# A two-layer encoder trunk: three of the second layer's four seven-product units get weight sums made on VectorE in the mLSTM layer and stored

## The chip, the core and the metric

One core of one Trainium2 chip runs the whole program. The time is device microseconds of an execution; "before" is the median of three runs.

## What is computed

Two layers over 256 positions of width 2048, all in float32. Layer 0 mixes by pooling and attention, layer 1 by a bidirectional mLSTM; each ends in a gated MLP with a width-3 convolution, which is where the change acts:

```python
def conv_ffn(x, w_up, conv_w, conv_b, w_down):
    u = x @ w_up
    up = jnp.pad(u, ((0, 0), (1, 1), (0, 0)))
    c = conv_w.astype(u.dtype)
    u = c[0] * up[:, :-2] + c[1] * up[:, 1:-1] + c[2] * up[:, 2:] + conv_b.astype(u.dtype)
    gate, val = jnp.split(u, 2, axis=-1)
    return (jax.nn.silu(gate) * val) @ w_down
...
for layer in range(DEPTH):
    h = rms_norm(x, norm_mix[layer])
    ...
    x = x + mixed
    x = x + conv_ffn(rms_norm(x, norm_ffn[layer]), w_up[layer], conv_w[layer], conv_b[layer], w_down[layer])
```

## The kernel before

All weights pass through one stream (`Stream`) of chunks, as a rule 128 partitions by 1024 floats (512 KB). SP loads a chunk into one of six raw buffers `w` (L93, L100; seven in the MLP). It is then split into a high part and a low part: ScalarE casts `w` to the high part (L164), VectorE subtracts that from `w` for the low part (L165); both stand in `hl`, of which there are four buffers (five in the MLP). TensorE takes three products for each weight block, high by high, high by low and low by high, all through the helper at L285. A chunk is 12 matmuls of 128x512 where the weights move, or 16 matmuls (eight of 512 columns and eight of 256) where they stand still. Loads are issued up to five chunks ahead (seven in the MLP) and splits two (three); the next load into a raw buffer waits until the last reader of that buffer is done, and SP works in order. The tile framework orders the instructions of VectorE, ScalarE, GpSimd and SP by a schedule of its own; TensorE's order is written out by hand.

The up-projection of the MLP has 44 tiles of gate and value columns, in six groups (`FCH`). Most tiles are plain (`up`). Four times in a layer, four tiles are done at once as a **unit** (`quads`): a product of 2 by 2 blocks with seven products for eight, which needs sums of activations and sums of weights. The activations' sums are made once a layer on VectorE and ScalarE (`sums`, L1003 to L1019). A unit has 28 chunks of six matmuls; they are woven into plain work, slot by slot (a slot is one plain chunk), by the table `UNITS`. An entry is (group, half, first slot, last slot, prepared or not). I call the four units of a layer first to fourth.

The weights' sums come in two ways. In a unit that is not prepared, VectorE adds inside the raw buffers before the split (`sums` of `Stream`, L144, L147, L149, L150), 32 adds of 128x512 a unit. In a prepared unit the sums lie in DRAM tiles `G`, eight pairs a unit, made ahead of time by DMAs alone: two copies DRAM to DRAM from SP (L118), two accumulating DMAs from GpSimd (L119) and two more within `G` (L123); `_make_steps` gives for each pair the load index at which its four steps go out. The chunks of a prepared unit are loaded from `G` and from the weights, as many bytes as otherwise.

In the mLSTM layer the stream feeds, for each of four head pairs, a value projection (tile `mv`), two query and two key projections (`mq`, `mk`) and an output-gate projection (`mo`), then the output projection (`op`, into which `mcat` goes). VectorE also does the gating: L904 and four reciprocals L906 for each head pair, then L910 and L920. The code holds, unused before, a third way to make sums: a pair of chunks marked "prep" in the stream (`_with_prep`, `is_prep`, `prepare`), which is loaded into two raw buffers, summed by four adds (L134) and stored to `G` by two DMAs from GpSimd (L135, L136).

Of the kernel before, what the change touches and what calls it, by code (L numbers as in the profile page):

```python
# [1241 lines left out]
def _down_chunks(w):  # L1242
# [6 lines left out]


UNITS = (
    ((2, 1, 18, 62, 0), (3, 1, 66, 94, 1), (4, 1, 98, 142, 0), (5, 1, 146, 174, 1)),
    ((2, 1, 18, 62, 0), (3, 1, 66, 94, 1), (4, 1, 98, 142, 0), (5, 1, 146, 174, 1)),
)


# [73 lines left out]
def _with_prep(seq, pairs, first, gap):  # L1330

    out = []
    for i, e in enumerate(seq):
        n, r = divmod(i - first, gap)
        if r == 0 and 0 <= n < len(pairs):
            key, q = pairs[n]
            out += [(("prep", 0, key), q[:, 0:1024]), (("prep", 1, key), q[:, 1024:2048])]
        out.append(e)
    return out


def _make_steps(pairs, places):

    make = {}
    for (key, q), (at, gap) in zip(pairs, places):
        for part in range(4):
            make.setdefault(at + part * gap, []).append((key, part, q))
    return make
# [105 lines left out]
```

## Time and profile before

| | |
|---|---|
| median of 3 runs | 2179.74 us (2179.56 to 2181.44) |
| profiled execution | 2179.59 us, of which 2177.8 us span of instructions |
| granted TensorE clock | 1.000 |
| TensorE, VectorE, ScalarE, GpSimd busy | 2164.5, 1711.6, 1277.6, 133.5 us |
| DMA | 533.18 MB, mean 245 GB/s |

The attention layer fills the span up to about 256 us, the first MLP up to 977, the mLSTM layer up to 1455, the second MLP the rest. In a line of groups stand source line, engine, operation, tiles written and read, count, busy time, mean of one in ns, then the engine's idle time before them and what ended it. In a list of waits stand the waiting engine, tile and line, then who ended the wait, with the total in us, the number of waits and the longest. A timeline row has start, length, engine, line, operation, tiles, count, and in brackets the idle time before it.

### The profile page before, as it was taken

To read this page: it belongs to the slowest core of one execution; us is meant where nothing else is said; L and a number is where in the kernel's file an instruction comes from. 1 tells how busy PE (TensorE), PEld (TensorE's weight loads), DVE (VectorE), ACT (ScalarE), POOL (GpSimd) and SP (SyncE) were. 2 spreads that over 40 slices of the span, in tenths; PEclk is the share of its full clock that TensorE was granted. 3 is DMA by queue.
4 is the path that set the end of the run, shared out by engine and by line. 5 is a ranking of instruction groups with operands and counts; after the bars stand their busy time and mean duration, and the time that the engine had idled before them with its cause. 6 is when DMAs were issued, how large, how long until landed. Compare 5 with 4: busy or idle time off the path is not lost.

```text
span 2177.8 us, 30504 instructions
## 1 busy us (share of the span) xinstructions
PE 2164.5 (99%) x11040; PEld 1838.1 (84%) x11040; DVE 1711.6 (79%) x2414; ACT 1277.6 (59%) x1808; POOL 133.5 (6%) x168
## 2 busy tenths in 40 slices
PE   9999999999999999999999999999999999999999
PEld 7888888888888888889888888888888888888887
DVE  7686699888798787866767676669888879979785
ACT  7665555666565575655555554556566656556663
POOL 0121101000000000001101010110000000000000
PEclk9999999999999999999999999999999999999999
DMA  8868879889978878769788777877876875767773
GB/s 324 245 217 249 236 234 295 276 264 293 301 235 287 272 232 250 262 202 253 219 248 226 238 229 219 265 223 222 269 244 223 258 247 202 258 232 233 251 232 126
DMA packets 157467, 533.18 MB, mean 245 GB/s; under 512 B 18715, under 2 KB 21059, under 8 KB 156291
## 3 DMA queue, kind: packets, MB, share of 16 engines
q1 hardware_dynamic: 139744, 493.66, 66.2%
q0 software_dynamic: 14496, 33.83, 10.5%
q10 hardware_dynamic: 3074, 3.75, 0.9%
q8 instruction: 86, 1.41, 0.3%
q14 instruction: 67, 0.54, 0.1%
HBM read 529.02 MB, written 69.25 MB: 275 GB/s over the span
## 4 chain that ended last, share of the span: by engine, by line
PE 92%; DVE 6%; issue 1%; ACT 1%; DMA 0%; ACTq 0%; SPq 0%; DVEq 0%
PE up L285 24%; PE dn L285 20%; PE p L285 13%; PE op L285 8%; PE mv L285 4%; PE mq L285 4%; PE mk L285 4%; PE mo L285 4%; PE qproj L285 3%; DVE hl L165 3%; PE pool L285 1%; PE vproj L285 1%; PE kproj L285 1%; ACT hl L164 1%; PE tr L1098 1%
## 5 line engine op out<-in xcount | busy, mean ns | idle before, releaser
L165 DVE TENSOR_TENSOR hl<-w,hl 128x1024 fp32r<-128x1024 f32 (+1 forms) x868 | 1045.0, 1216 | 334.9 <-ACT hl L164 328.1
L164 ACT CAST hl<-w 128x1024 fp32r<-128x1024 f32 (+1 forms) x867 | 897.7, 1048 | 643.7 <-PE up L285 115.8
L285 PE MATMUL up<-xx,hl 128*128 128x512 f32 (+1 forms) x3584 | 647.8, 337 | 0.0
L285 PEld LDWEIGHTS up<-xx,hl 128*128 128x128 f32 x3584 | 563.4, 188 | 87.7 <-DVE hl L165 0.4
L285 PE MATMUL dn<-hl,g 128*128 128x512 f32 x2064 | 492.7, 391 | 0.0
L285 PEld LDWEIGHTS dn<-hl,g 128*128 128x128 f32 x2064 | 385.2, 188 | 78.5
L285 PE MATMUL p<-hl,sx 128*128 128x512 f32 x768 | 206.7, 391 | 3.5 <-DVE hl L165 2.5
L285 PEld LDWEIGHTS p<-hl,sx 128*128 128x128 f32 x768 | 139.4, 188 | 30.6 <-DVE hl L165 3.8
L285 PE MATMUL p<-hl,xx 128*128 128x512 f32 x576 | 157.9, 391 | 4.6 <-DVE hl L165 4.6
L285 PEld LDWEIGHTS p<-hl,xx 128*128 128x128 f32 x576 | 104.5, 188 | 25.3 <-DVE hl L165 6.3
L119 POOL DMA_DIRECT2D G<-in_q x64 | 52.2, 816 | 984.7 <-DMA G<-in_q 972.8
L285 PE MATMUL mk<-xx,hl 128*128 128x512 f32 (+1 forms) x512 | 92.2, 338 | 0.0
L285 PE MATMUL mq<-xx,hl 128*128 128x512 f32 (+1 forms) x512 | 92.2, 338 | 0.0
L285 PE MATMUL mv<-hl,xx 128*128 128x512 f32 (+2 forms) x480 | 91.8, 351 | 0.0
L285 PE MATMUL op<-hl,cat 128*128 128x512 f32 x384 | 91.7, 394 | 0.0
L285 PE MATMUL mo<-hl,xx 128*128 128x512 f32 x384 | 90.6, 392 | 0.0
L285 PE MATMUL op<-hl,mcat 128*128 128x512 f32 x384 | 89.5, 392 | 0.0
L285 PEld LDWEIGHTS mq<-xx,hl 128*128 128x128 f32 x512 | 79.3, 188 | 11.5
L285 PEld LDWEIGHTS mk<-xx,hl 128*128 128x128 f32 x512 | 79.1, 188 | 11.3
L285 PEld LDWEIGHTS mv<-hl,xx 128*128 128x128 f32 x480 | 78.3, 189 | 11.2
L285 PEld LDWEIGHTS op<-hl,mcat 128*128 128x128 f32 x384 | 71.5, 188 | 14.6
L285 PEld LDWEIGHTS mo<-hl,xx 128*128 128x128 f32 x384 | 71.0, 188 | 14.2
(243 smaller groups left out, 1860.8 us busy)
## 6 DMA issues: line engine op xcount, KB each, us to landing
w<-in_up SPq DMA_DIRECT2D x224, 512.0 KB, 4.7
w<-in_dn SPq DMA_DIRECT2D x176, 512.0 KB, 4.6
w<-in_m_in SPq DMA_DIRECT2D x124, 512.0 KB, 5.2
w<-in_q SPq DMA_DIRECT2D x96, 512.0 KB, 4.8
G<-in_q SPq DMA_DIRECT2D x64, 512.0 KB, 5.7
w<-in_a_in SPq DMA_DIRECT2D x46, 512.0 KB, 6.1
G<-in_q POOLq DMA_DIRECT2D x64, 256.0 KB, 6.4
G<-G POOLq DMA_DIRECT2D x64, 256.0 KB, 7.2
```

What stands on the lines that cost most here:

```text
L119: pin(add.dma_start(G[r, 0:1024], src[r, 512:1536], accum_op=ALU.add))
L164: (self.nc.vector.tensor_copy if i + c == 0 else self.nc.scalar.copy)(hl[:, 0, c : c + n], w[:, c : c + n])
L165: self.nc.vector.tensor_sub(hl[:, 1, c : c + n], w[:, c : c + n], hl[:, 0, c : c + n].bitcast(F32))
L285: pe.matmul(out_, lhsT, rhs, start=start, stop=stop, skip_group_check=True)
L1098: pe.transpose(tr[:, j, t * P : t * P + P], src[:, c : c + P], ident)
```

## The change

Which units are prepared changes in both layers, and how they are prepared in layer 1. In layer 0 the second and fourth were prepared; now the first and third are, as before by DMAs alone, issued at other loads (in the attention layer and in the first third of the MLP). In layer 1 the second and fourth were prepared by DMAs; now the first, second and fourth are, by the "prep" chunks: 24 pairs, one pair ahead of every seventh chunk of the mLSTM layer's stream, from its first. The DMAs that made layer 1's sums between the end of the first MLP and the second are gone. The slots of the units move.

```diff
 UNITS = (
-    ((2, 1, 18, 62, 0), (3, 1, 66, 94, 1), (4, 1, 98, 142, 0), (5, 1, 146, 174, 1)),
-    ((2, 1, 18, 62, 0), (3, 1, 66, 94, 1), (4, 1, 98, 142, 0), (5, 1, 146, 174, 1)),
+    ((2, 1, 18, 57, 1), (3, 1, 61, 101, 0), (4, 1, 105, 131, 1), (5, 1, 135, 174, 0)),
+    ((2, 1, 18, 57, 1), (3, 1, 61, 90, 1), (4, 1, 94, 140, 0), (5, 1, 144, 174, 1)),
 )
...
     weights = att + ffn(0)
-    make = _make_steps(pairs[0], [(24 + 11 * k, 5) for k in range(8)] + [(len(att) + 30 + 24 * k, 12) for k in range(8)])
-    make.update(_make_steps(pairs[1], [(len(weights) - 20 + 14 * k, 7) for k in range(16)]))
-    weights = weights + ml + ffn(1)
+    make = _make_steps(pairs[0], [(24 + 10 * k, 5) for k in range(8)] + [(len(att) + 24 + 17 * k, 8) for k in range(8)])
+    weights = weights + _with_prep(ml, pairs[1], 0, 7) + ffn(1)
```

Three places in the order of instructions follow. First, VectorE at the start of the first unit of layer 1, before:

```order
L144 TENSOR_TENSOR w_13317<-w_13317 128x512
L1009 TENSOR_TENSOR v_13136<-v_13136 128x512
L1010 TENSOR_TENSOR v_13136<-v_13136 128x512
L982 TENSOR_TENSOR y_2_13305<-y_2_13305 128x256
L1012 SCALAR_TENSOR_TENSOR v_13136<-v_13136 128x512
L165 TENSOR_TENSOR hl_13429<-w_13317,hl_13429 128x1024
L1013 TENSOR_TENSOR v_13136<-v_13136 128x512
L450 TENSOR_TENSOR tb_up_3_13410<-up_3_13316,tb_up_3_13410 128x512
L165 TENSOR_TENSOR hl_13452<-w_13340,hl_13452 128x1024
L149 TENSOR_TENSOR w_13363<-w_13363,w_13317 128x512
```

The same engine and place now (`sx` and `v` are the activations' sums, `w` a raw chunk, `hl` its split):

```order
L1019 TENSOR_TENSOR sx_13116<-v_13304,sx_13116 128x4x128
L450 TENSOR_TENSOR tb_up_3_13571<-up_3_13480,tb_up_3_13571 128x512
L165 TENSOR_TENSOR hl_13614<-w_13505,hl_13614 128x1024
L1019 TENSOR_TENSOR sx_13116<-v_13304,sx_13116 128x4x128
L984 TENSOR_TENSOR g_0_13124<-y_2_13469,g_0_13124 128x256
L1014 TENSOR_TENSOR v_13304<-v_13304 128x512
L1019 TENSOR_TENSOR sx_13116<-v_13304,sx_13116 128x4x128
L165 TENSOR_TENSOR hl_13638<-w_13528,hl_13638 128x1024
L994 TENSOR_TENSOR tb_up_3_13571<-tb_up_3_13571,R_13239 128x512
L165 TENSOR_TENSOR hl_13659<-w_13550,hl_13659 128x1024
```

The adds into `w` (L144, L149) are gone from the place; the activations' sums stay.

Second, VectorE after the output-gate projection of the third head pair in the mLSTM layer, before:

```order
L165 TENSOR_TENSOR hl_11431<-w_11348,hl_11431 128x1024
L297 TENSOR_TENSOR re_h_11397<-re_h_11397,ry_h_11395 128x2
L904 TENSOR_SCALAR og_11440<-og_11440 128x2x256 x2
L906 RECIPROCAL og_11440<-og_11440 128x256 x2
L165 TENSOR_TENSOR hl_11453<-w_11365,hl_11453 128x1024
L906 RECIPROCAL og_11440<-og_11440 128x256
L165 TENSOR_TENSOR hl_11471<-w_11410,hl_11471 128x1024
L165 TENSOR_TENSOR hl_11493<-w_11429,hl_11493 128x1024
```

And now:

```order
L165 TENSOR_TENSOR hl_11535<-w_11500,hl_11535 128x1024
L297 TENSOR_TENSOR re_h_11487<-re_h_11487,ry_h_11485 128x2
L134 TENSOR_TENSOR w_11399<-w_11399 128x512
L134 TENSOR_TENSOR w_11399<-w_11399,w_11416 128x512
L134 TENSOR_TENSOR w_11416<-w_11416,w_11399 128x512
L904 TENSOR_SCALAR og_11544<-og_11544 128x2x256 x2
L134 TENSOR_TENSOR w_11416<-w_11416 128x512
L906 RECIPROCAL og_11544<-og_11544 128x256 x3
L165 TENSOR_TENSOR hl_11557<-w_11523,hl_11557 128x1024
L906 RECIPROCAL og_11544<-og_11544 128x256
L165 TENSOR_TENSOR hl_11575<-w_11528,hl_11575 128x1024
```

The four adds of a pair stand around L904, and three reciprocals, not two, come ahead of the next subtract.

Third, VectorE after the output-gate projection of the second head pair, now (the pair in `w_10638` and `w_10657`; `w_10830` is the chunk that is loaded into the buffer of `w_10638`):

```order
L910 TENSOR_TENSOR hn_10358<-hn_10358,og_10668 128x512
L134 TENSOR_TENSOR w_10638<-w_10638 128x512
L165 TENSOR_TENSOR hl_10745<-w_10712,hl_10745 128x1024
L165 TENSOR_TENSOR hl_10773<-w_10733,hl_10773 128x1024
L906 RECIPROCAL og_10668<-og_10668 128x256
L134 TENSOR_TENSOR w_10638<-w_10638,w_10657 128x512
L165 TENSOR_TENSOR hl_10791<-w_10738,hl_10791 128x1024
L920 SCALAR_TENSOR_TENSOR mcat_8748<-htr_10760,cst,mcat_8748 128x256
L910 TENSOR_TENSOR hn_10618<-hn_10618,og_10668 128x512
L134 TENSOR_TENSOR w_10657<-w_10657,w_10638 128x512
```

Nothing of these adds stood there before; `w_10638` is final after the second of them and can then be stored.

## The prediction

> **What bounds the kernel now.** I read the page's busy times and chain first, then who the weight loads of TensorE wait for, then the windows around those waits.
>
> ```profile
> PE 2164.5 (99%) x11040; PEld 1838.1 (84%) x11040; DVE 1711.6 (79%) x2414; ACT 1277.6 (59%) x1808; POOL 133.5 (6%) x168
> PE 92%; DVE 6%; issue 1%; ACT 1%; DMA 0%; ACTq 0%; SPq 0%; DVEq 0%
> ```
>
> TensorE carries 92% of the chain that ended last, and the change takes no matmul away: both versions have four units in each layer. So only TensorE's waits can be won. A matmul's modelled end hides a part of each wait; the weight load's row shows it better. Waits of the weight loads, in four windows in this order: 300 to 400 us (first unit of layer 0, three rows), 600 to 700 (its third unit), 1500 to 1600 (first unit of layer 1, two rows), 1800 to 1900 (its third unit).
>
> ```profile
> PEld p L285 <- DVE hl L165: 2.7, 4, 1.1
> PEld p L285 <- ACT hl L164: 0.5, 1, 0.5
> PEld up L285 <- DVE hl L165: 0.4, 1, 0.4
> ...
> PEld p L285 <- DVE hl L165: 1.7, 1, 1.7
> ...
> PEld p L285 <- DVE hl L165: 4.5, 4, 2.0
> PEld p L285 <- ACT hl L164: 0.9, 1, 0.9
> ...
> PEld p L285 <- DVE hl L165: 1.2, 1, 1.2
> ```
>
> That is 3.6, 1.7, 5.4 and 1.2 us, **11.9 us in all, the ceiling of any gain**. Every one stands in the first third of a unit whose sums are made on the spot; the two prepared units of each layer show none. Is that VectorE being full, or the sums themselves? Three windows of 24 us and the mLSTM layer (columns: length, then busy us of PE, PEld, DVE, ACT, POOL, clock, DMA share, GB/s):
>
> ```profile
> 472.00:496.00 24.00, 24.00 (x130) 20.42 (x129) 23.14 (x40) 18.73 (x32) 1.64 (x2) 1.00 0.91 270
> 352.00:376.00 24.00, 24.00 (x126) 20.48 (x126) 22.34 (x28) 14.68 (x19) 1.61 (x2) 1.00 0.96 312
> 1840.00:1864.00 24.00, 23.15 (x112) 19.28 (x111) 21.10 (x27) 13.70 (x17) 0.00 (x0) 1.00 0.67 227
> 976.00:1454.00 478.00, 478.00 (x2572) 412.49 (x2571) 330.67 (x512) 247.61 (x339) 46.13 (x59) 1.00 0.81 237
> ```
>
> At 472 us a prepared unit follows the unit before it with VectorE at 23.14 of 24 us, and TensorE does not wait; at 1840 us VectorE has less to do (21.10) and TensorE loses 0.85. So it is the chain add, ACT cast, VectorE subtract, each queued behind other work, and not occupancy alone. The mLSTM layer has no wait of TensorE, with VectorE at 331 of 478 us.
>
> **The first units (both layers).** Prepared, they load finished sums: no add stands ahead of a cast. By the prepared unit at 472 us such a start costs nothing, though here the sums of the activations (L1003 to L1019) run beside it. I take 0; bounds 0 and half of the old wait. Gain: 5.4 in layer 1 and 3.6 in layer 0. What is late next there is the cast behind the ring of split buffers, which TensorE itself empties.
>
> **The other units.** Layer 1 has its unprepared unit at the same place, in 46 slots for 44: 0. In layer 0 the third unit becomes prepared (gain 1.7) and the second and the fourth become unprepared, each starting four slots after the unit before it, as the old third did. Nearest rows 1.7 and 1.2: I take 1.7 each, 3.4. They are packed tighter (40 and 39 slots for 44), so the upper bound is the first unit's 3.6 each, the lower 1.2. Layer 0: 3.4 - 3.6 - 1.7 = **-1.9**. Layer 1: **-5.4**.
>
> **The mLSTM layer: adds.** Each of 24 pairs brings four adds of 128x512; the old sums' rows price one:
>
> ```profile
> L147 DVE TENSOR_TENSOR w<-w 128x512 f32<-128x512 f32 x32 | 21.9, 683 | 0.0
> ```
>
> 96 x 0.683 = 65.6 us on an engine with 478 - 331 = 147 us free: on the average it is hidden. It is not where TensorE's lookahead is short, after an output-gate projection. Third head pair, VectorE, then ACT, then PE:
>
> ```profile
> 1269.96 0.76 DVE L904 TENSOR_SCALAR og<-og 128x512 f32<-128x512 f32 x2 [2.12 <-ACT og L900]
> 1270.64 3.35 DVE L906 RECIPROCAL og<-og 128x256 f32<-128x256 f32 x2
> 1273.91 1.16 DVE L165 TENSOR_TENSOR hl<-w,hl 128x1024 fp32r<-128x1024 f32 x1
> 1274.99 1.74 DVE L906 RECIPROCAL og<-og 128x256 f32<-128x256 f32 x1
> 1276.65 3.42 DVE L165 TENSOR_TENSOR hl<-w,hl 128x1024 fp32r<-128x1024 f32 x3
> ...
> 1269.80 2.11 ACT L164 CAST hl<-w 128x1024 fp32r<-128x1024 f32 x2
> 1273.57 1.06 ACT L164 CAST hl<-w 128x1024 fp32r<-128x1024 f32 x1 [1.67 <-PE mv L285]
> ...
> 1267.93 13.77 PE L285 MATMUL mv<-hl,xx 128*128 128x512 f32 x60
> 1281.54 0.60 PE L915 MATMUL htr<-cst,hn 128*128 128x128 f32 x4
> ```
>
> A chunk is 12 matmuls, so five chunks pass from 1267.93 to 1281.54, 2.72 us each; they start at 1267.93, 1270.65, 1273.37, 1276.10 and 1278.82. The cast at 1273.57 takes the buffer that the second chunk left, so it is the sixth; the two casts at 1269.80 are the fourth and fifth. The fourth's subtract ends at 1273.91 + 1.16 = 1275.07, **1.03 us before TensorE needs it**; the fifth's at about 1277.8, 1.0 before. The order of the changed kernel puts one add and a third reciprocal ahead of that first subtract here: 0.68 + 1.68 (half of 3.35) - 1.03 = 1.3 us of wait. At the fourth head pair an add and a reciprocal stand there too: 1.3. At the first, three adds (2.05) fall into the 2.12 us idle ahead of L904 and one costs 0.68 of the 1.03; at the second, none is there. Sum **+2.6**, bounds 0 and 10 (below).
>
> **The mLSTM layer: stores.** Two of the six raw buffers now stay taken until a store to DRAM lands, and the load that takes them next stands in SP's queue with all later loads behind it. Nearest rows for load and store:
>
> ```profile
> w<-in_m_in SPq DMA_DIRECT2D x124, 512.0 KB, 5.2
> G<-in_q POOLq DMA_DIRECT2D x64, 256.0 KB, 6.4
> G<-G POOLq DMA_DIRECT2D x64, 256.0 KB, 7.2
> out<-x SPq DMA_DIRECT2D x3, 512.0 KB, 3.1
> L123 POOL DMA_DIRECT2D G<-G x64 | 59.1, 923 | 177.7 <-DMA G<-in_q 132.7 <-DMA G<-G 38.7 <-issue 6.2
> ```
>
> The tightest place I found in the projections is the pair whose first tile is final after the last reciprocal of the second head pair; its buffer goes to the fourth chunk of the next query projection:
>
> ```profile
> 1185.89 1.74 DVE L906 RECIPROCAL og<-og 128x256 f32<-128x256 f32 x1
> ...
> 1194.36 2.24 PE L285 MATMUL mq<-xx,hl 128*128 128x512 f32 x12
> 1196.43 0.60 PE L915 MATMUL htr<-cst,hn 128*128 128x128 f32 x4
> 1196.79 9.32 PE L285 MATMUL mq<-xx,hl 128*128 128x512 f32 x52
> ```
>
> The tile is final at 1185.89 + 1.74 + 0.68 = 1188.3. Of 16 matmuls a chunk, four remain at 1196.79; at 9.16/52 = 0.176 us each the fourth chunk starts at 1196.79 + 36 x 0.176 = 1203.1. Room 14.8. Needed: issue 0.92, landing 3.1 to 7.2, load 5.2, cast and subtract 1.05 + 1.16: 11.4 to 15.5. So it fits or misses by 0.7; the others, as I followed them through the order and the trace, have 1.5 us more room or better, but for one in the output projection. I take 0, and 6.4 as the landing. [...]
>
> **DMA share.** Queues in 976 to 1454 us, then in 300 to 600:
>
> ```profile
> q1 hardware_dynamic: 24331, 98.43, 59.2%
> q0 software_dynamic: 5376, 12.46, 18.1%
> ...
> q1 hardware_dynamic: 22079, 76.91, 72.9%
> q0 software_dynamic: 2859, 6.60, 14.0%
> ```
>
> In the mLSTM layer 24 + 24 copies of 0.52 MB go in as loads and out as stores. At q1's price (59.2% for 98 MB) the loads replace 12.5 MB of copies and make 67%, the stores 15%: 82% for 81% now. At q0's price the stores alone take 37%: 104%. In layer 0 pairs are made every 17 loads instead of 24, so 14.0% becomes 19.8% and q1 some 75%: 95%. The window at 352 us shows 0.96 with TensorE never waiting; I take 0, bounds 0 and 5.
>
> **Sum.** -5.4 - 1.9 + 2.6 = -4.7. The profiled execution took 2179.59 (span 2177.8 and 1.8 around it), by 0.15 under the median 2179.74. Forecast **2174.9**.
>
> **Rivals.**
> 1. *Slower: the stores hold the raw buffers.* Decides when issue to landing is over some 8 us, at a DMA share near 100%. With the whole path 3 us longer than its upper end (18.5 for 14.8) that place loses 3.7 us; if one place in each head pair and in the output projection does, 5 x 3.7 = 18.5 less the gain of 7.3: about 2191. For it: q0's price. Against: 3.1 us for a plain store.
> 2. *The new unprepared starts in layer 0 cost as the old first one did:* 3.6 each, 3.8 more: 2178.7. For it: the tighter packing; against: the activations' sums are not beside them.
> 3. *The first units wait all the same,* because the activations' sums crowd VectorE: half of 9.0 stays, 4.5 more: 2179.4. The change then does not do what it says. Against it: the window at 472 us.
> 4. *The adds hide entirely and the new starts cost 1.2:* -5.4 - 2.9 = -8.3: 2171.3.
>
> **How the numbers follow.** Forecast 0.55, rivals 0.16, 0.11, 0.09, 0.09 in this order. About 0.2% (4.4 us) can be told from no change, so the line lies at 2175.4. Of the forecast's own spread, 2171 to 2179, some two thirds lie below it: 0.36, with rival 4 0.45 faster; the rest with rivals 2 and 3 is 0.39; slower 0.16. The range: below, all waits but two starts of 1.2 gone, 2170.0; above, the slow rival in part, with DMA bounds (5) and a few places of the stores, 2185.0.
>
> **What would show it.** Right: no wait of the weight loads in the first 100 us of a unit in layer 1 but at its third; waits of 1 to 2 us at the second and fourth unit of layer 0; waits of about 1.3 us behind the output-gate projections of the third and the fourth head pair, by the subtract; stores that land in under 7 us. Wrong: waits on loads in the mLSTM layer, a DMA share there over 0.95, or waits in layer 0 spread over all of 300 to 600 us.

## The result and the profile after

The changed kernel takes **2197.93 us** (median of 4, 2196.76 to 2199.42), the one before on the same chip 2179.8: a ratio of 1.0082, interval 1.0064 to 1.0099. It is slower by 0.8%, above my range (2170 to 2185) and on the side that I had given 0.16. The profiled execution took 2198.37 us, 18.8 more than that of before. Its page shows:

```profile
PE 2172.4 (99%) x11040; PEld 1841.7 (84%) x11040; DVE 1752.4 (80%) x2478; ACT 1281.6 (58%) x1808; POOL 108.5 (5%) x152
PE 89%; DVE 4%; DMA 3%; issue 3%; ACT 1%; POOL 0%; DVEq 0%; ACTq 0%; POOLq 0%; SPq 0%
```

The same 11040 matmuls, but 3% of the chain is now DMA, where before it was 0%. That already speaks against my step on the stores, but only a run without them can price it.

Where the 18.8 us went needs a measure that the modelled ends of matmuls don't blur. I use **lost time**: for each matmul, how much later the next one starts than is the median after a matmul of that shape, added up over a stage. Before, 33.5 us are lost in the whole program, now 52.4: the difference of 18.9 is the difference in time.

| lost TensorE time, us | layer 0 MLP (300 to 960) | mLSTM (960 to 1455) | layer 1 MLP (from 1455) |
|---|---|---|---|
| before | 9.4 | 5.2 | 11.4 |
| after | 15.8 | 19.8 | 9.0 |

Who the weight loads of TensorE wait for, in the windows of the prediction: 300 to 400, 600 to 700 and 1500 to 1600 us show no row at all any more. The other windows of the changed kernel, in this order: 500 to 600 (second unit of layer 0), 750 to 850 (its fourth, which begins at 758.8 us), 1800 to 1900 (third unit of layer 1), 980 to 1460 (mLSTM).

```profile
PEld p L285 <- ACT hl L164: 2.3, 1, 2.3
PEld p L285 <- DVE hl L165: 1.7, 2, 1.3
...
PEld p L285 <- ACT tb L1100: 2.7, 1, 2.7
PEld p L285 <- DVE hl L165: 2.1, 1, 2.1
...
PEld p L285 <- ACT tb L1100: 2.3, 1, 2.3
...
PEld htr L915 <- DVE hn L910: 4.5, 2, 3.4
...
PEld gtr L781 <- ACT gn L775: 1.7, 1, 1.7
...
PEld mv L285 <- DVE hl L165: 1.3, 1, 1.3
PEld op L285 <- DVE hl L165: 1.2, 1, 1.2
```

The gains came as forecast: the first units and the third unit of layer 0 wait no more. The two units of layer 0 that are now unprepared cost more than forecast, and not all of it at their starts. In the order of TensorE's matmuls the waits stand at the sixteenth of the second unit's 28 chunks, and at the second chunk (for a PSUM bank that ACT's copy L1100 frees) and the fourteenth of the fourth unit. The prepared third unit, 636 to 743 us, does not wait. In the mLSTM layer, which had no wait, eight kinds of wait appeared, four of which are shown. Two of them, `mv` and the first of `htr`, are at the third head pair; `op` and the second `htr`, 3.15 us later than it should be, stand in the output projection.

What the waits of the mLSTM layer are made of is seen on the engines behind it. SP's queue (which issues the loads) and ACT, same window:

```profile
SPq L100 <- DVE hl L165: 225.7, 111, 7.0
SPq L100 <- DMA G<-w: 122.3, 41, 6.1
...
ACT hl L164 <- DMA w<-in_m_in: 45.1, 21, 6.3
```

In 41 cases a load stood in SP's queue until a store (`G<-w`) had landed, 122.3 us in all; before, no load waited for a DMA there. That is no price by itself: SP's queue stood still for 402.1 us before and for 403.6 now, since waits for VectorE (336.7 us before) gave way to waits for stores. What counts is ACT's casts. They waited 45.1 us for loads of the projections and 17.6 for those of the output projection, before 1.5 in all. (In layer 0's MLP, 300 to 960 us, no cast waited for a load.) The stores were no slower than I took them to be:

```profile
G<-w POOLq DMA_DIRECT2D x48, 512.0 KB, 5.3
...
980.00:1460.00 480.00, 469.91 (x2516) 402.84 (x2515) 375.28 (x596) 239.63 (x331) 33.57 (x57) 1.00 0.81 275
```

They land in 5.3 us, for the 6.4 that I had taken, and the DMA share is 0.81 (forecast 0.82). So the store's own time and the share were no worse than forecast. One thing that I had not followed holds buffers longer, GpSimd's order at the start of the layer:

```profile
1000.86 0.58 POOL L371 DMA_DIRECT2D R<-rr  x1 [10.83 <-DMA rr<-re_n]
1001.43 0.54 POOL L135 DMA_DIRECT2D G<-w  x1
```

`R<-rr` waits 10.83 us for a 1 KB bounce through DRAM (`rr<-re_n`), and the stores of the second pair stand behind it in GpSimd's order. The first tile of that pair was final at 995.2 us and goes out at 1001.4. That TensorE paid for this is not shown: its wait `gtr` at 1001 us goes back to a cast that stood still for 5.38 us, for a load that SP had issued at 989.66, ahead of these stores; and in a second execution of the same kernel (after_again, below) `gtr` does not wait.

And VectorE ahead of the largest single wait, `htr` in the output projection:

```profile
1383.42 3.36 DVE L906 RECIPROCAL og<-og 128x256 f32<-128x256 f32 x2
1386.70 0.63 DVE L134 TENSOR_TENSOR w<-w 128x512 f32<-128x512 f32 x1
...
1392.24 0.68 DVE L134 TENSOR_TENSOR w<-w,w 128x512 f32<-128x512 f32 x1
...
1393.98 0.68 DVE L134 TENSOR_TENSOR w<-w,w 128x512 f32<-128x512 f32 x1
...
1395.71 1.75 DVE L906 RECIPROCAL og<-og 128x256 f32<-128x256 f32 x1
1397.38 0.63 DVE L134 TENSOR_TENSOR w<-w 128x512 f32<-128x512 f32 x1
1397.92 0.68 DVE L910 TENSOR_TENSOR hn<-hn,og 128x512 f32<-128x512 f32 x1
...
1398.66 0.55 PE L915 MATMUL htr<-cst,hn 128*128 128x128 f32 x3 [2.99 <-DVE hn L910]
```

In the rows left out are another reciprocal and five subtracts; from 1382.75 us to the end of L910 VectorE is never idle. The four adds (0.63 to 0.68 each, 2.6 together) stand ahead of L910, on which TensorE waits 2.99 us. Locally VectorE is full, though over the layer it has some 100 us free (375.28 of 480 busy).

The last part is the clock. The trace of before shows full clock from 4.3 us to its end. The changed one shows four stretches of 3.413 us at half clock, each right after a wait. Two pairs of windows, a wait and what follows it (columns as in the prediction; the clock is the third number from the end):

```profile
544.00:547.42 3.42, 1.58 (x6) 1.09 (x7) 2.59 (x4) 0.84 (x1) 0.00 (x0) 1.00 1.02 317
547.42:550.83 3.41, 3.41 (x12) 2.84 (x11) 2.21 (x3) 1.04 (x1) 0.00 (x0) 0.50 1.11 450
...
1393.90:1397.31 3.41, 1.76 (x8) 1.13 (x6) 3.41 (x4) 1.34 (x2) 0.00 (x0) 1.00 0.77 216
1397.31:1400.72 3.41, 2.06 (x11) 1.80 (x12) 3.41 (x6) 0.73 (x2) 0.53 (x1) 1.00 1.00 410
```

In these four stretches a matmul of 128x512 starts 427 ns after the one before it, in place of 227 (medians of that trace). By an estimate from the granted clock of 0.50, half of 3.413 us is the most that each can cost: 4 x 1.7 = 6.8 of the 18.8 us. By lost time it is some 1.5: layer 0 loses 15.8 us here and 12.8 in the run l1_before, which has the same waits and no stretch. Not every wait brings one: the 2.99 us before `htr` lie across two windows, in which TensorE is busy 1.76 and 2.06 us, and the clock stays at 1.00. A run below, and the last section, show what goes with it.

### The profile page after: what moved, and what is told of

Its sections match the earlier page's. It is cut to its first block, busy times and chain, and to the rows that moved or that the text cites. A ratio compares the mean times of both kernels' runs of the same rounds, so it can differ in the third digit from the quotient of the medians.

```text
span 2196.6 us, 30694 instructions
## 1 busy us (share of the span) xinstructions
PE 2172.4 (99%) x11040; PEld 1841.7 (84%) x11040; DVE 1752.4 (80%) x2478; ACT 1281.6 (58%) x1808; POOL 108.5 (5%) x152
## 4 chain that ended last, share of the span: by engine, by line
PE 89%; DVE 4%; DMA 3%; issue 3%; ACT 1%; POOL 0%; DVEq 0%; ACTq 0%; POOLq 0%; SPq 0%
PE up L285 28%; PE dn L285 21%; PE p L285 14%; PE op L285 7%; PE qproj L285 3%; PE mk L285 3%; PE mq L285 2%; PE mo L285 2%; DVE hl L165 2%; PE mv L285 2%; DMA w<-in_m_in 1%; PE kproj L285 1%; PE vproj L285 1%; DMA w<-in_q 1%; ACT hl L164 1%
## 5 line engine op out<-in xcount | busy, mean ns | idle before, releaser
L285 PEld LDWEIGHTS up<-xx,hl 128*128 128x128 f32 x3584 | 569.6, 189 | 90.0
L285 PEld LDWEIGHTS mk<-xx,hl 128*128 128x128 f32 x512 | 79.1, 188 | 11.4
L285 PEld LDWEIGHTS op<-hl,mcat 128*128 128x128 f32 x384 | 71.4, 188 | 15.8 <-DVE hl L165 1.2
L285 PEld LDWEIGHTS op<-hl,cat 128*128 128x128 f32 x384 | 70.9, 188 | 14.1
```

Of the source, the lines that this page charges most:

```text
L285: pe.matmul(out_, lhsT, rhs, start=start, stop=stop, skip_group_check=True)
```

## The experiments

The theories after reading the two traces: the halves of the change cost apart from each other; in the mLSTM layer it is either the **stores** (raw buffers held, loads late) or the **adds** (in VectorE's fixed order ahead of what TensorE needs); and the half-clock stretches come on top, by chance or by the waits. All runs are compared with the kernel before on the same chip, whose median there was 2180.4 to 2181.4. The lost time of each, in one table (stretches: number of 3.413 us windows at half clock before the last 30 us of the profiled execution; last column: what ACT's casts waited for loads from 980 to 1460 us). The stages are cut at the same times in every run. The scheduler orders VectorE anew for each of these kernels, so a difference is that of the edit together with the order that came of it:

| run | layer 0 MLP | mLSTM | layer 1 MLP | stretches | casts for loads, us |
|---|---|---|---|---|---|
| before | 9.4 | 5.2 | 11.4 | 0 | 1.5 |
| after | 15.8 | 19.8 | 9.0 | 4 | 62.7 |
| l0_before | 9.5 | 17.3 | 7.4 | 0 | 69.9 |
| l1_before | 12.8 | 5.3 | 11.5 | 0 | 1.4 |
| no_stores | 9.5 | 13.0 | 7.4 | 0 | 11.2 |
| no_adds | 9.5 | 9.8 | 7.4 | 0 | 13.2 |
| no_both | 9.5 | 7.3 | 8.9 | 1 | 3.8 |
| adds_free | 9.5 | 13.3 | 8.9 | 2 | 4.0 |
| dma3 | 9.5 | 6.4 | 6.9 | 0 | 2.8 |
| later | 9.5 | 31.1 | 9.0 | 7 | 84.8 |
| pool_adds | 9.5 | 32.8 | 7.4 | 7 | 8.4 |
| moved | 9.5 | 35.6 | 9.0 | 6 | 131.6 |
| three | 21.2 | 6.3 | 7.8 | 2 | 3.6 |
| l0_gap | 19.9 | 6.7 | 11.3 | 4 | 6.3 |
| after_again | 12.8 | 19.5 | 9.0 | 2 | 52.4 |
| l0_buf7 | 9.5 | 25.0 | 9.0 | 2 | 36.4 |
| moved_buf7 | 9.5 | 59.7 | 9.1 | 11 | 91.9 |

**Each half alone.** l0_before takes layer 0 back:

```diff
-    ((2, 1, 18, 57, 1), (3, 1, 61, 101, 0), (4, 1, 105, 131, 1), (5, 1, 135, 174, 0)),
+    ((2, 1, 18, 62, 0), (3, 1, 66, 94, 1), (4, 1, 98, 142, 0), (5, 1, 146, 174, 1)),
-    make = _make_steps(pairs[0], [(24 + 10 * k, 5) ... (len(att) + 24 + 17 * k, 8) ...
+    make = _make_steps(pairs[0], [(24 + 11 * k, 5) ... (len(att) + 30 + 24 * k, 12) ...
```

> The changed kernel with layer 0 (its table row and its makes) as before; the mLSTM layer and layer 1 as changed. The windows of the changed kernel's trace show 14.5 us more lost TensorE time in the mLSTM layer, 5.6 less at layer 1's first unit and 2.7 more at its third. Theory, two separate causes: this half alone costs 14.5 - 5.6 + 2.7 = 11.6, so about 2191.4 us. Rival, the halves act on each other (the mLSTM layer starts late or with full queues because layer 0 ended otherwise): the waits at 1001 to 1046 us go as well and the time is 2184 or less.

l1_before takes the other half back (layer 1's row, its makes by DMAs, no `_with_prep`).

> The kernel before with layer 0 (its table row and its makes) as changed; the mLSTM layer and layer 1 as before. The windows show 3.4 and 1.5 us less lost at the first and third unit of layer 0 and 5.1, 3.9 and 2.0 more around 542, 763 and 824 us: +6.1, so about 2185.8 us; with the half-clock stretches at 547 and 766 us again. My prediction's step for this half gave -1.9, so 2177.8. If two separate causes is right, this excess and that of the other half add up to 18.2.

Measured: l0_before 2190.40 us against 2181.44, ratio 1.0048 [1.0035, 1.0062]; l1_before 2188.20, ratio 1.0032 [1.0020, 1.0044]. The two excesses, 9.0 and 6.8, sum to 15.8; the ratios to 1.0080, as the whole change. By lost time of the whole program the halves' profiled executions, without half clock, lost 8.2 and 4.5 us more than before, and the whole change 18.9 with up to 6.8 of half clock. So two separate causes, and the rival of halves that act on each other falls. The forecasts were 11.6 and 6.1 above before, measured are 9.0 and 6.8. I had expected the half clock to come with l1_before's waits; its profiled execution has the waits and no half-clock stretch:

```profile
PE p L285 <- ACT tb L1100: 2.3, 1, 2.3
PE p L285 <- ACT hl L164: 2.1, 1, 2.1
```

These are the largest single waits of TensorE itself from 500 to 850 us, the first at the fourth unit's second chunk and the other at the second unit's sixteenth; the time of that execution, 2183.84, is 4.4 below the median of its kind.

**Adds or stores.** Based on l0_before, no_stores drops the two DMAs of `prepare` and lets layer 1 load from the input; no_adds drops the four adds; no_both drops both.

```diff
-        for to, other in ((b11, b12), (b12, b22), (b22, b11), (b21, b22)):
-            pin(add(to, to, other))
-        self.nc.gpsimd.dma_start(G[:, 0:1024], x)
-        self.nc.gpsimd.dma_start(G[:, 1024:2048], w)
```

> As the run with layer 0 as before, but the sums made on VectorE are not stored; layer 1's prepared units load raw blocks of the same sizes from the input instead of the sums, so their products are of other numbers. Loads and adds of the mLSTM layer stay. Theory stores (they hold raw buffers and stand in POOL's queue behind the wait for a small DRAM bounce, so later loads and casts are late): the mLSTM layer loses only the 2.6 us that I had put down to the adds, the time is about 2179.7 - 5.6 + 2.7 + 2.6 = 2179.4. Rival adds (they stand in VectorE's order ahead of the subtracts and ACT's casts wait in line): nothing changes, 2190 to 2191.

> As the run with layer 0 as before, but the 96 additions on VectorE are left out: the raw blocks are loaded and stored as they are, so layer 1's prepared units multiply other numbers. Loads and stores of the mLSTM layer stay. Theory stores: only the adds' small share goes, 2188 to 2190. Rival adds: the mLSTM layer loses nothing more, 2179.7 - 5.6 + 2.7 = about 2177.

> As the run with layer 0 as before, without the adds and without the stores: the 48 loads of the mLSTM layer stay and are read by nothing, layer 1's prepared units load raw blocks of the same sizes. If adds and stores are all of the mLSTM layer's cost, it loses nothing more than before there, and what is left is layer 1: -5.6 + 2.7 = 2.9 us faster than before. Rival, the loads themselves cost (DMA share, raw buffers taken for a load's time): the time stays within 1 us of the run without adds, 0.9 faster than before.

Measured: no_stores 2185.43 (1.0019 [1.0010, 1.0028]), no_adds 2180.57 (0.9996 [0.9987, 1.0005]), no_both 2179.11 against 2180.41 (0.9990 [0.9981, 1.0000]). Neither theory alone holds. From the table, in the mLSTM layer: the loads with the order that came with them cost 2.1 us (5.2 to 7.3), stores without adds 2.5 more, adds without stores 5.7 more, both together 10.0 more. The waits of TensorE in that layer, first without stores, then without adds, then without both (lines stand two or four higher, since the edits take lines out):

```profile
PE htr L913 <- DVE hn L908: 3.7, 2, 3.0
PE mv L283 <- DVE hl L163: 0.9, 1, 0.9
PE op L283 <- DVE hl L163: 0.8, 1, 0.8
```

```profile
PE qk L283 <- DVE hl_k L824: 1.0, 1, 1.0
PE htr L913 <- DVE hn L908: 0.7, 1, 0.7
```

```profile
PE htr L911 <- DVE hn L906: 0.7, 1, 0.7
PE mv L281 <- DVE hl L161: 0.3, 1, 0.3
PE op L281 <- DVE hl L161: 0.2, 1, 0.2
```

Without the stores `htr`, `mv` and `op` wait exactly as in l0_before (3.7, 0.9, 0.8). What goes beyond the third list, 3.0 at `htr` and 0.6 each at `mv` and `op`, is the adds'. The third list itself, most of the 2.1 us, comes neither from the adds nor from late loads: no cast waits for a load of the layer there, but at the third head pair three reciprocals, not two, come ahead of VectorE's next subtract. The waits at the start of the layer need stores: `qk` waits 1.0 and 0.4 without the adds, 0.3 without the stores, 2.2 with both, and `gtr` (1.1 in l0_before) waits only where both are there. The last column of the table says the same of the late loads: 13.2 us with the stores alone, 11.2 with the adds alone, 69.9 with both. A load is late where adds make a pair's tile final late and its buffer must then wait for the store as well; that order of causes is argued.

**Is it VectorE's time, or its standing still for the pair's loads?** In adds_free, which has no stores either, the additions work on a tile of zeros of their own:

```diff
-        x, G = self.first, self.made_tile(kind[2])
+        x, w = self.free or (self.first, w)
```

> As the run without stores (4.0 above before), with the additions done on a tile of zeros of their own in place of the loaded blocks (all but those of pairs ahead of the layer's start), so that VectorE never stands still for the loads of a pair (4.7 us in 3 waits there) and a raw buffer is free as soon as its load has landed. Nothing made by them is used. Theory, VectorE's time in its fixed order: the waits at the gated product (3.7 us) and before the value and output projections (0.9 and 0.8) stay, 3 to 4 above before. Rival, standing still for loads: they go, and the time is that of the run without adds and stores, 1.3 below before.

Measured 2184.64 (1.0017 [1.0007, 1.0026]), 4.2 above before, as without stores:

```profile
PE htr L916 <- DVE hn L911: 3.0, 1, 3.0
PE mv L283 <- DVE hl L163: 1.2, 2, 0.9
```

So the adds cost by the time they take in VectorE's order. By lost time the mLSTM layer has 13.3 us for 13.0, but one half-clock stretch is among them; without it the layer loses some 11.6 to 11.8, so 1.2 to 1.4 of the 5.7 us may come from standing still for loads.

**Can they stand elsewhere?** later starts the pairs 18 tiles on and puts one every 6; moved puts them only beside the query and key projections and the first output-gate tiles; pool_adds does them on GpSimd.

```diff
-    weights = weights + _with_prep(ml, pairs[1], 0, 7) + ffn(1)
+    weights = weights + _with_prep(ml, pairs[1], 18, 6) + ffn(1)
...
-        pin, add = self.tc.keep_in_program_order, self.nc.vector.tensor_add
+        pin, add = self.tc.keep_in_program_order, self.nc.gpsimd.tensor_add
```

> As the run with layer 0 as before, but the first pair stands 18 weight tiles later and a pair comes every 6 tiles. Theory, the waits at 1001 to 1046 us come from the store that POOL issues behind its wait for the small DRAM bounce at the layer's start: they go (5 to 6 us with what follows), those around the output-gate projections and the output projection stay, so some 5 above before. Rival, adds and stores cost wherever they stand: 9 above before, as that run, or more since they are denser.

> As the run with layer 0 as before (loads, adds and stores as changed), but the 24 pairs stand six to a head pair, four tiles apart, among the tiles of the query and key projections and the first of the output gate, none from the last tiles of the output gate to the first query projection of the next head pair, where VectorE has the reciprocals of the gate, and none in the output projection. Theory, an add costs only where it stands in VectorE's order among the reciprocals ahead of what TensorE waits for: the waits of the transposes for the gated product and of the value and output projections go, and the time is within 2 us of before. Rival, adds and stores cost wherever they stand: 9 us above before, or more, since the pairs are denser.

> As the run with layer 0 as before, with the 96 additions on GpSimd in place of VectorE; the loads and stores stay. Theory, the cost lies in VectorE's order (adds and reciprocals ahead of the subtract or the product that TensorE waits for): the waits around the output-gate projections and in the output projection go, some 2 us from the stores at the layer's start stay, so within 1 us of before, as without adds. Rival, the cost is the longer hold of the raw buffers: GpSimd takes longer for an add than VectorE, so the stores are later still and the time is 9 above before or more. A slowdown of VectorE itself while GpSimd adds would show in the mean of its subtracts (1.16 to 1.22 us).

Measured: later 2203.24 (1.0101 [1.0087, 1.0115]), moved 2206.51 (1.0117 [1.0103, 1.0131]), pool_adds 2203.33 (1.0100 [1.0086, 1.0114]). All three are far worse than l0_before (6, 5 and 7 stretches of half clock in the mLSTM layer are part of it), and my theory that only the place beside the reciprocals is dear falls. In later the waits at the start of the layer did go, as its theory said (the first loss of over 0.25 us is now at 1040 us), but `htr` lost 8.3 us at the first head pair and 7.8 in the output projection. TensorE's waits in the mLSTM layer, for later, moved (with ACT's) and pool_adds in turn:

```profile
PE htr L915 <- DVE hn L910: 15.7, 2, 8.1
```

```profile
PE atr L875 <- DVE A L867: 12.0, 4, 3.9
...
ACT hl L164 <- DMA w<-in_m_in: 131.4, 68, 6.2
```

```profile
PE mv L285 <- DVE hl L165: 7.6, 3, 4.2
```

In moved the reciprocals are clear of adds, and the small products `A` of each head pair wait instead: ACT's casts wait 131 us for loads. One timeline of moved, VectorE, then ACT:

```profile
1147.32 1.23 DVE L165 TENSOR_TENSOR hl<-w,hl 128x1024 fp32r<-128x1024 f32 x1 [1.24 <-ACT hl L164]
...
1149.59 0.34 DVE L867 SCALAR_TENSOR_TENSOR A<-arg,denr,A 128x128 f32<-128x128 f32 x1
...
1146.24 1.05 ACT L164 CAST hl<-w 128x1024 fp32r<-128x1024 f32 x1 [4.68 <-DMA w<-in_m_in]
```

The subtract of a weight that TensorE needs only later stands ahead of the product that it needs now; its cast waited 4.68 us for a late load, and so everything behind it waits. In pool_adds VectorE itself gets slower, in its group of the window 1000 to 1440 us:

```profile
L165 DVE TENSOR_TENSOR hl<-w,hl 128x1024 fp32r<-128x1024 f32 x139 | 191.6, 1386 | 51.8 <-ACT hl L164 50.9
L294 DVE TENSOR_TENSOR re_h<-ry_h 128x2 f32<-128x2 f32 x8 | 9.0, 1122 | 6.7 <-POOL ry_h L292 6.7
```

The subtract takes 1386 ns in the mean for 1217 before, and an operation on 128x2 elements 1122 ns for 160. VectorE is slower in this run, where GpSimd adds, and GpSimd took 1.5 to 1.8 us for an addition in place of 0.68, so the pairs' buffers were held longer as well; but the casts waited only 8.4 us for loads, so late loads are not what cost here.

**One raw buffer more.** l0_buf7 and moved_buf7 give the mLSTM layer a seventh raw buffer.

> As the run with layer 0 as before, with seven raw buffers in the mLSTM layer for six. Theory hold (a store that has not landed keeps a raw buffer, the next load is late, and so are cast and subtract): ACT's waits on the loads of the layer, 53.3 us in 25 in that run, fall to under half, the mLSTM layer's lost TensorE time falls from 17.3 towards the 13.0 of the run without stores, the time to 5 to 7 above before from 9. Rival, VectorE's order alone: the waits on loads change, the time does not by more than 1 us.

> As the run with the pairs moved among the query and key projections (26 above before), with seven raw buffers in the mLSTM layer for six. Theory hold: there ACT waited 131 us in 68 for loads, and VectorE's subtract of a late tile stood ahead of the small products that TensorE waits for (A, 12.0 us); with one buffer more these waits fall to under half and the time by 10 us or more. Rival, the additions in VectorE's order: the 12.0 us stay within 3, and the time too.

Measured 2196.81 (1.0083 [1.0058, 1.0108]) and 2234.86 (1.0248 [1.0230, 1.0265]), 16 and 54 above before: both missed, and both theories with them. ACT's waits on the layer's loads did fall (in l0_buf7 from 53.3 to 30.4 us for those of the projections), but the order of VectorE's instructions, which the scheduler makes anew, differs as well, and new waits came (`mv` 3.5, `mk` 2.0). The edit is not clean, so how much of the cost a larger ring would take away stays open.

**Layer 0.** l0_gap starts each unit eight slots after the one before it:

```diff
-    ((2, 1, 18, 57, 1), (3, 1, 61, 101, 0), (4, 1, 105, 131, 1), (5, 1, 135, 174, 0)),
+    ((2, 1, 18, 55, 1), (3, 1, 63, 99, 0), (4, 1, 107, 131, 1), (5, 1, 139, 174, 0)),
```

> As the run with only layer 0 changed (6.8 above before), but each unit starts eight slots after the end of the unit before it and not four, in shorter stretches (37, 36, 24 and 35 slots for 39, 40, 26 and 39). Theory, the new waits of layer 0 are those of a start right behind the finish of a unit, where ACT's copies of the transposes, VectorE's additions and the casts crowd: the 2.3 us wait for a PSUM bank at the third unit goes, those at the second and fourth shrink, and the time is within 2 us of before. Rival, it is the unprepared units' packing, which gets denser here: 7 above before or more.

Measured 2192.64 (1.0054 [1.0040, 1.0068]), 12 above before: by its number the rival. The wait for the PSUM bank is gone (it was the fourth unit's, not the third's as I had it), the other waits of the two unprepared units are worse, 500 to 850 us:

```profile
PE p L285 <- ACT hl L164: 5.5, 2, 3.5
PE p L285 <- DVE hl L165: 4.7, 3, 2.6
```

By lost time it is 19.9 for 12.8 in l1_before, and 6.8 of these 7.1 are four half-clock stretches. So without half clock the sum is about the same: what the fourth unit no longer waits at its second chunk, it waits at its sixth (3.6 and 2.2 us), and the second unit waits more at its sixteenth (2.2 and 2.9 for 2.2 and 1.2), in shorter stretches (36 and 35 slots). That the density of their sums is the reason fits, but no run here varies it alone.

**The sums by DMAs.** dma3 keeps the changed table of layer 1 with its three prepared units, and has the sums made by accumulating DMAs; layer 0 as before. three does that in layer 0 as well.

```diff
-    weights = weights + _with_prep(ml, pairs[1], 0, 7) + ffn(1)
+    make.update(_make_steps(pairs[1], [(len(weights) - 20 + 10 * k, 5) for k in range(24)]))
+    weights = weights + ml + ffn(1)
```

> Layer 0 as before. Layer 1 with the changed table (three prepared units), but their sums made as before, by accumulating DMAs, a pair every 10 loads in place of 14. No adds on VectorE, no extra loads through the raw buffers. Theory (adds and stores cost, the table of layer 1 gains): the mLSTM layer shows no wait, layer 1's first unit none, so -5.6 + 2.7 = about 2.9 us faster than before, or up to 5 if the third unit's start differs. Rival, DMA share: 24 pairs in this stretch take q0 from 18% to 25% and the mLSTM layer to about 0.9; then waits on loads appear in the layer and the time is that of before or above.

> Both layers with three prepared units (first, second and fourth, the changed table's row of layer 1), all sums made by accumulating DMAs: layer 1's as in the run that had them so (4.7 below before), layer 0's a pair every 9 loads from the 24th load on. Theory, a prepared unit that starts a layer gains wherever its sums come from: 3.4 more in layer 0, so 8.1 below before. Rival, DMA: the pairs of layer 0 now lie where the share was 0.72 to 0.93; with a pair every 9 loads it goes to 1, loads come late, and the time is that of before or above.

Measured: dma3 **2175.68** against 2180.41, ratio 0.9976 [0.9967, 0.9985]: faster than both kernels. Its mLSTM layer has 1.2 us more lost time than before and its layer 1 4.5 us less. The DMA share there, 976 to 1454 us, and the largest wait of its weight loads in layer 1:

```profile
976.00:1454.00 478.00, 477.19 (x2567) 411.13 (x2566) 330.22 (x511) 246.30 (x339) 60.15 (x75) 1.00 0.88 254
...
PEld p L285 <- ACT tb L1100: 1.6, 1, 1.6
```

three took 2188.16 (1.0035 [1.0024, 1.0047]), above before as the DMA rival had it. A stretch of its layer 0:

```profile
350.00:450.00 100.00, 100.00 (x521) 85.42 (x520) 75.26 (x94) 59.69 (x76) 15.31 (x19) 1.00 1.03 331
```

With the share at 1.03, and 1.04 in the next 100 us, casts wait on loads (82.8 us from 300 to 960), and 11.7 us more are lost in the layer (up to 3.4 of it at half clock), though its first unit no longer waits. TensorE is still never idle in the stretch shown; it loses from 454 us on. The largest single loss, 4.15 us, is the wait for a PSUM bank at the second chunk of the third unit, which cost 1.4 in dma3's layer 1; how much of it late loads made is not shown. At 0.88 the same means cost 1.2.

**The clock.** after_again is the changed kernel, unchanged.

> The changed kernel once more. The trace in hand has four stretches of 3.413 us at half clock, after waits of about 2 us or several smaller ones, and they cost about 1.7 us each. Theory, it is chance which wait falls into a window of the clock's gate: the same waits within 0.3 us at the same places, but another number of half-clock stretches, and a time that is lower by 1.7 for each one fewer. Rival, a wait of 2 us always brings one: the same four.

Measured 2195.40 and 2201.86 us in two executions; the profiled one has two half-clock stretches, not four. The waits in the MLPs are the same to 0.05 us by lost time (2.24, 1.22, 2.42, 1.85, 2.05). At the start of the mLSTM layer they are not: `gtr` lost 1.7 us in the first trace and nothing in this one, `mv` 3.0 in this one and nothing in the first. The two waits of layer 0 and the one before `htr`, in windows of its grid:

```profile
541.60:545.02 3.42, 1.64 (x11) 1.26 (x9) 3.42 (x4) 3.07 (x4) 0.00 (x0) 1.00 0.98 207
...
763.47:766.88 3.41, 1.97 (x10) 1.67 (x11) 3.37 (x9) 1.82 (x3) 0.00 (x0) 1.00 0.79 235
...
1391.55:1394.96 3.41, 0.86 (x6) 0.82 (x7) 3.41 (x4) 1.00 (x2) 0.53 (x1) 1.00 0.97 352
1394.96:1398.37 3.41, 3.41 (x10) 2.62 (x9) 1.70 (x4) 0.78 (x2) 0.00 (x0) 0.50 1.01 388
```

The two waits in layer 0 that had halved the clock don't here; the one before `htr` now does. For the clock the theory holds by these two traces: the same waits, but another choice of those that bring a stretch (a window is in the traces one cell of a 3.413 us grid). How is in "What the runs showed of the hardware", below.

## Why the prediction was wrong, step by step

- **The first units and the old third of layer 0: right.** The waits of 3.6, 1.7 and 5.4 us are gone; dma3 shows the gain by itself.
- **The place of the waits: misread.** I wrote that every wait stands in the first third of its unit. Of the 5.4 us at the first unit of layer 1, 2.1 (1580 to 1600 us: 1.2 by VectorE and 0.9 by ACT) stand at its sixteenth chunk, in its middle. So I priced starts alone.
- **The new unprepared units of layer 0 at 1.7 each: the step that failed there.** By lost time the second cost 3.5 (2.24 and 1.22), none of it at its start but at the same sixteenth chunk. The fourth cost 4.3: 2.42 at its second chunk, whose PSUM bank was freed by ACT's copy L1100, part of finishing the third unit, which itself had waited 1.11 us for VectorE; and 1.85 at its fourteenth. That is 7.7 for 3.4. Against -1.9 stand +3.4 (9.4 to 12.8 in l1_before, without half clock). The upper bound, 3.6, was right for the second unit only. I had priced a unit by who waits for the sums at its start, and not by all that stands in line on ACT and VectorE.
- **The third unit of layer 1 at 0:** its wait rose from 1.2 by the weight loads to 2.3, and changed to a PSUM bank at its second chunk, as in the fourth unit of layer 0.
- **The adds at +2.6: the places right, the size half.** At the third head pair I forecast 1.3 before the subtract and got 1.03; 0.79 came at `htr` too, but no_both loses that (0.82) without adds. At the fourth I counted an add and a reciprocal ahead of the first subtract, and 0.97 came there; I did not follow the order to L910, ahead of which three more adds stand, 3.15. Without stores the adds cost 5.7 (7.3 to 13.0); adds_free shows that most of it is VectorE's time.
- **The stores at 0: wrong.** They cost 2.5 by themselves and 4.3 (13.0 to 17.3) beside the adds. The landing, 5.3 us, was within the 6.4 that I took. What I had put at nothing is that with the adds ahead of it a store makes the next loads late: my own sign of being wrong, waits on loads in the mLSTM layer, came with 62.7 us of ACT's casts (69.9 in l0_before, 13.2 without the adds). I had followed buffers in the middle of the layer, one add's end, a landing and a load in a row; I left out GpSimd's order at the start (10.83 us behind a bounce) and what a late cast and subtract stand in front of. Which of these made most of the 4.3 stays open.
- **The pairs' loads, not in the sum:** with the scheduler's order that came with them they cost 2.1 (no_both).
- **The DMA share at 0: right** in size (0.81) and by dma3 in cost (0.88 there, 1.2 us).
- **Not in the sum: the clock.** Four stretches, at most 6.8 us in the profiled execution.

In sum: layer 0 +6.4 with 3.0 of half clock (15.8 against 12.8), the mLSTM layer +14.6 with up to 1.7, layer 1 -2.4 with up to 1.7 against it; 0.3 are ahead of them. The largest error is the mLSTM layer, put at +2.6, where adds, stores and the order around the loads cost 12.1 (5.2 to 17.3 in l0_before). The slower rival (about 2191, chance 0.16) was right that the stores hold buffers, but its conditions did not come (a landing over 8 us, a share near 100%; measured 5.3 and 0.81); that l0_before, 2190.4, is close to its time is luck, by another sum.

## What to carry to other kernels

Work that fills an engine's free time on the average must still be placed in a fixed order, and there each operation of it, and each wait of it, stands ahead of something that another engine waits for: read the order as far as the last such consumer, not to the first. If transfers have room (0.81 to 0.88 here, not 1.03), sums made by accumulating DMAs cost less here than sums on an engine in whose order they can stand badly (1.2 us of lost time in the mLSTM layer of dma3, 12.1 in l0_before). And a wait of 2 us may cost up to 3.7, by an estimate (2 + 1.7): one of 2.05 us was followed here by 3.413 us at a granted clock of 0.50.

## What the runs showed of the hardware

The half-clock stretches lie on a grid. In the changed kernel they begin at 547.42, 765.88, 1045.77 and 1827.42 us: 64, 82 and 229 times 3.413 us apart, and in each of the other traces the same way. A long wait was not needed for one: the wait ahead of the stretch at 1827.42 us, for ACT's copy L1100, is 2.05 us by lost time (1.9 in the row of TensorE's own waits).

What goes with them in these traces is how long TensorE is busy (by the profile's modelled ends) within one window of the grid. I laid the grid over the eleven traces that have a half-clock stretch, and took all windows at full clock in which it was busy less than 2.6 of 3.413 us: 34 windows with up to 1.59 us were all followed by half clock, 61 windows with 1.60 us or more were not, without exception. Two near the bar are in the fences above, 544.00 us of the first trace (1.58) and 541.60 us of the second (1.64): the same wait, cut by the grid at two places. At half clock the bar lies higher: windows busy up to 2.48 us kept it there, those with 2.89 us or more did not, but for one of pool_adds (1017.73 us) that was busy throughout and kept it too. So what ends half clock is not settled. Where the grid lies differs from one execution to the next (bounds at 544.00 and 541.60 us in these two, 2.40 us apart), and so the times of one kernel with such waits scatter (2195.40 and 2201.86 in after_again), while those of before, without, lie within 0.2%. That the scatter of times that have no trace comes from this alone is argued, not shown.
